# The opening of a hybrid decoder layer rebuilt: token sums from a token-major copy on ScalarE, the first two weight chunks together by quarters, one store on another queue

## The chip, the cores and the metric

The kernel runs on one core of one Trainium2 chip. The metric is device time in microseconds (us); lower is better. The core's engines are TensorE (PE; PEld is its weight load), VectorE (DVE), ScalarE (ACT), GpSimd (POOL) and SyncE (SP, which here only issues DMA). They run side by side and wait for each other by semaphores.

## The reference, cut to what matters

One layer over 272 tokens (16 learned meta tokens and 256 inputs) of width 2048, in float32:

```python
hn = rmsnorm(h_res, norm_g[l])          # x * rsqrt(mean(x*x) + eps) * g, token by token
p = hn @ w_in[l]                        # 2048 x 22528, by column blocks:
# glu_a | glu_b | conv_gate | q | k | v | ret_gate | merge_a | merge_b
y_a = conformer_branch(glu_a, glu_b, conv_gate, ...)   # glu, causal conv of 31 taps, layernorm, @ conv_out
o = retention_chunkwise(qf, kf, v)                     # 8 heads, with per-head decay
y_b = (groupnorm(o) * silu(ret_gate)) @ ret_out[l]
merged = sigmoid(merge_a) * y_a + sigmoid(merge_b) * y_b
h_res = h_res + merged @ w_out[l]
y = rmsnorm(h_res, final_norm_g)[:, N_META:]
```

## The kernel before

**Weights as a stream.** All weights pass once, as chunks of 128 x 2048 float32 (1 MB), in the order of the list `seq`. For each chunk SP loads `raw` (three buffers), `split` cuts it in two parts for a float32 product in three passes (`whi` on ScalarE and `wlo` on VectorE, three buffers each; a buffer comes free when TensorE is done with the chunk that it held), and TensorE multiplies it. A chunk of the input projection gives 128 columns for all tokens, in one PSUM bank of the pool `accp`, which has four; the bank comes free when VectorE has read it. Chunks are counted from 0 here. Chunks 0 and 1 are glu gates, 2 and 3 glu values (all four by `project`, 272 tokens, 48 matmuls), chunk 4 is the first of q (by `project_wide`).

**The input.** `x_sb` holds x with channels on the partitions, as 16 groups of 128 channels. It comes in four quarters, each with a quarter of chunk 0. `hn` is x times the gain `ng`, cut in two parts (L145 on ScalarE, L146 on VectorE). The factor per token, rsqrt(mean of squares), is not in `hn`: it is multiplied in when a product is read from PSUM, from the tile `row`.

**The factor per token** is made beside the first chunks: squares on ScalarE (L154), sums over 16 groups on VectorE (L155, L158, `part`), sums over partitions as three small products with `ones` (`token_sums`, L172), the power -1/2 on GpSimd (L103, `rcol`). `token_row` spreads it over all partitions by products with `ident` (L183, L184), copies it to `row` (L185) and multiplies the rotary table `cs_sb` with it (L186). What reads the products of chunks 0 to 2 from PSUM (`evac`, for chunk 0 the line L265) is held back until then:

```python
        evac = seq[i][1](*parts.pop(i))
        if i < 3:
            held.append(evac)
        ...
        elif i == 2:
            token_row()
            ...
            for evac in held:
                evac()
```

**Order.** A scheduler places the instructions of each engine, near the order of the code; every engine then runs its own list in that order, and an instruction that waits holds up all that stand behind it on its engine. At the end `finish` scales two blocks of 128 tokens and stores each in four pieces from SP (L661).

Of the kernel before, what the change touches and what calls it, by code (L numbers as in the profile page):

```python
# [10 lines left out]
F32 = mybir.dt.float32  # L11
# [25 lines left out]
def hybrid_kernel(ctx: ExitStack, tc, xt, xnat, gain, par, fg, cs, dec, win, cout, rout, wout, out):  # L37
# [78 lines left out]
    x_sb = xin.tile([P, KT, L], F32, name="x_sb")  # L116
    sq = xin.tile([P, KT, L], F32, name="sq")
    part = xin.tile([P, CH, L], F32, name="part")
# [4 lines left out]

    def pre_norm():
        """x * g, transposed and split; the first chunk of weights; the sums of squares."""
        hi = stage.tile([P, D], F32R, tag="whi", name="whi", bufs=SPLITS)
        lo = stage.tile([P, D], F32R, tag="wlo", name="wlo", bufs=SPLITS)
        parts[0] = (hi, lo)
        raw = raws[0] = stage.tile([P, D], F32, tag="raw", name="raw", bufs=LOADS)
        n = KT // CH  # L130
        for c in range(CH):
            s = slice(c * n, (c + 1) * n)
            nc.sync.dma_start(out=x_sb[:, s], in_=xt[:, s])
            w = slice(c * 512, (c + 1) * 512)
            nc.sync.dma_start(out=raw[:, w], in_=seq[0][0][:, w])
        load(1, 2)
        nc.sync.dma_start(out=par_sb, in_=par)
        nc.sync.dma_start(out=cs_sb, in_=cs)
        for i in range(2, LOADS):
            load(i)  # L140
        for c in range(CH):
            s = slice(c * n, (c + 1) * n)
            w = slice(c * 512, (c + 1) * 512)
            for k in range(c * n, (c + 1) * n):
                nc.scalar.activation(out=hn_hi[:, k], in_=x_sb[:, k], func=AF.Copy, scale=ng[:, k:k + 1])  # L145
                nc.vector.scalar_tensor_tensor(out=hn_lo[:, k], in0=x_sb[:, k], scalar=ng[:, k:k + 1],  # L146
                                               in1=hn_hi[:, k].bitcast(F32), op0=ALU.mult, op1=ALU.subtract)
            split(raw[:, w], hi[:, w], lo[:, w])
        raws.pop(0)

    def part_sums():
        n = KT // CH
        for c in range(CH):
            nc.scalar.activation(out=sq[:, c * n:(c + 1) * n], in_=x_sb[:, c * n:(c + 1) * n], func=AF.Square)  # L154
            nc.vector.tensor_reduce(out=part[:, c], in_=sq[:, c * n:(c + 1) * n].rearrange("p k t -> p t k"),  # L155
                                    op=ALU.add, axis=mybir.AxisListType.X)
            if c:
                nc.vector.tensor_tensor(out=part[:, 0], in0=part[:, 0], in1=part[:, c], op=ALU.add)  # L158

    def last32(pool, a, n):  # L160
        """The last 32 tokens of a, three times over."""
# [4 lines left out]

    def token_sums():
# [5 lines left out]
        nc.gpsimd.memset(cols, 1.0)  # L173
# [3 lines left out]
        for t in range(3):  # L177
            nc.vector.tensor_copy(out=lhs[:, t], in_=rcol[:, t:t + 1].broadcast_to([P, P]))
# [10 lines left out]
    def project(acc, hi, lo, group=KT):  # L189
        """acc[:, :L] = (128 columns of the chunk).T @ input, all tokens."""  # L190
        for c in range(0, KT, group):
            for k in range(c, c + group):
                w = hi[:, k * P:(k + 1) * P]
                nc.tensor.matmul(acc[:, 0:L], lhsT=w, rhs=hn_hi[:, k], start=(k == 0), stop=False)  # L194
                nc.tensor.matmul(acc[:, 0:L], lhsT=w, rhs=hn_lo[:, k], start=False, stop=False)  # L195
            for k in range(c, c + group):
                nc.tensor.matmul(acc[:, 0:L], lhsT=lo[:, k * P:(k + 1) * P], rhs=hn_hi[:, k],  # L197
                                 start=False, stop=(k == KT - 1))
# [11 lines left out]
    def halves(acc, out):  # L210
        """out = the sum of both halves of acc."""
# [4 lines left out]
    def contract(acc, hi, lo, a_hi, a_lo, kts, col):  # L216
        """acc = sum over kts of w[:, kt, col block].T @ a[:, kt]."""
# [581 lines left out]
```

## Time and the profile before

| | us |
|---|---|
| median of three runs | 1461.59 |
| lowest and highest run | 1460.44, 1461.92 |
| span of the profiled execution | 1460.0 |
| TensorE busy in it | 1441.5 |
| first matmul | 7.63 |
| first matmul of chunk 4 | 43.44 |

The profile gives the profiled execution by its span, from the first to the last instruction; what lies around the span is not shown. That span is 1.59 us under the median of the runs. Times of the trace are counted from the start of the span.

### The profile page before, as it was taken

The page shows a single profiled execution, that of the slowest core. Times are in us where ns is not written, and L with a number is a line of the kernel's source. Part 1 is how long each engine was busy: PE and PEld are TensorE (multiplying, and loading weights), DVE is VectorE, ACT ScalarE, POOL GpSimd, SP SyncE. Part 2 cuts the span into 40 slices and gives each one's busy share as a digit, 9 for nine tenths or more (in the row PEclk, how much of TensorE's full clock was granted, in tenths as well). Part 3 has the DMA queues.
Part 4 walks back from the last instruction along what each step waited for, and adds up shares of the span by engine and source line. Part 5 has one row for each costly group of instructions (what it writes and reads, how often), then busy time and mean ns, then how long its engine had stood idle before and what let it go on. Part 6 is the DMA issues. An engine that isn't in the chain of part 4 may idle for free.

```text
span 1460.0 us, 23130 instructions
## 1 busy us (share of the span) xinstructions
PE 1441.5 (99%) x9790; PEld 1339.5 (92%) x9790; DVE 1080.3 (74%) x1475; ACT 685.7 (47%) x833; POOL 9.4 (1%) x24
## 2 busy tenths in 40 slices
PE   7999999999999999999999999999999999999997
PEld 6999999999999999999999999989888888888886
DVE  7987956985895696689579569757878876666553
ACT  6445446344435534534443453454456654444433
POOL 0000000000000000000000000000000000000000
PEclk9999999999999999999999999999999999999999
DMA  7645454555455455455455455545455555555752
GB/s 267 210 164 174 173 184 171 173 178 176 154 194 173 160 176 199 149 173 199 153 174 182 172 173 173 174 155 192 173 195 180 187 188 190 186 186 189 287 177 84
DMA packets 38839, 263.38 MB, mean 180 GB/s; under 512 B 4432, under 2 KB 4432, under 8 KB 8016
## 3 DMA queue, kind: packets, MB, share of 16 engines
q1 hardware_dynamic: 37152, 256.59, 51.3%
q10 hardware_dynamic: 1584, 5.32, 1.0%
q8 instruction: 77, 1.26, 0.3%
q14 instruction: 26, 0.21, 0.0%
HBM read 259.79 MB, written 2.10 MB: 179 GB/s over the span
## 4 chain that ended last, share of the span: by engine, by line
PE 97%; DVE 1%; ACT 1%; issue 0%; DMA 0%; ACTq 0%; POOLq 0%; POOL 0%
PE ps L208 29%; PE ps L206 14%; PE ps L194 11%; PE ps L195 11%; PE ps L197 11%; PE ps L223 4%; PE ps L220 4%; PE ps L221 4%; PE ps L594 2%; PE ps L597 2%; PE ps L593 2%; PE ps L374 0%; PE ps L434 0%; ACT hn L145 0%; DVE part L155 0%; PE ps L410 0%
## 5 line engine op out<-in xcount | busy, mean ns | idle before, releaser
L51 DVE TENSOR_TENSOR wlo<-raw,whi 128x2048 fp32r<-128x2048 f32 (+2 forms) x244 | 549.9, 2254 | 171.5 <-ACT whi L50 144.8
L50 ACT ACTIVATE whi<-raw 128x2048 fp32r<-128x2048 f32 (+2 forms) x244 | 460.6, 1888 | 303.1 <-PE ps L195 122.4
L208 PE MATMUL ps<-hn,whi 128*128 128x512 f32 x1536 | 384.4, 397 | 0.0
L208 PEld LDWEIGHTS ps<-hn,whi 128*128 128x128 f32 x1536 | 285.5, 189 | 59.0
L194 PE MATMUL ps<-hn,whi 128*128 128x272 f32 x1280 | 328.9, 292 | 7.7 <-ACT whi L50 7.6
L195 PE MATMUL ps<-hn,whi 128*128 128x272 f32 x1280 | 327.3, 289 | 0.0
L194 PEld LDWEIGHTS ps<-hn,whi 128*128 128x128 f32 x1280 | 243.0, 190 | 8.1 <-ACT whi L50 8.0
L195 PEld LDWEIGHTS ps<-hn,whi 128*128 128x128 f32 x1280 | 243.2, 190 | 1.1
L252 DVE SCALAR_TENSOR_TENSOR c_sb<-u,par_sb,c_sb 128x256 f32<-128x256 f32 x480 | 205.9, 480 | 1.5
L206 PEld LDWEIGHTS ps<-hn,wlo 128*128 128x128 f32 x1536 | 194.8, 189 | 8.9
L206 PE MATMUL ps<-hn,wlo 128*128 128x256 f32 x1536 | 197.1, 282 | 0.0
L197 PE MATMUL ps<-hn,wlo 128*128 128x272 f32 x1280 | 172.7, 287 | 0.5 <-DVE wlo L51 0.4
L213 ACT COPY half<-ps 128x256 f32<-128x256 f32 x112 | 41.6, 372 | 280.1 <-PE ps L208 280.1
L197 PEld LDWEIGHTS ps<-hn,wlo 128*128 128x128 f32 x1280 | 164.4, 188 | 1.1 <-DVE wlo L51 1.1
L220 PE MATMUL ps<-zhi,whi 128*128 128x256 f32 x512 | 125.9, 280 | 0.0
L221 PE MATMUL ps<-zlo,whi 128*128 128x256 f32 x512 | 125.9, 280 | 0.0
L221 PEld LDWEIGHTS ps<-zlo,whi 128*128 128x128 f32 x512 | 96.3, 188 | 0.0
L220 PEld LDWEIGHTS ps<-zhi,whi 128*128 128x128 f32 x512 | 96.2, 188 | 0.0
L223 PE MATMUL ps<-zhi,wlo 128*128 128x256 f32 x512 | 80.9, 280 | 0.0
L223 PEld LDWEIGHTS ps<-zhi,wlo 128*128 128x128 f32 x512 | 69.1, 188 | 0.0
L208 PE MATMUL ps<-s,whi 128*128 128x512 f32 x256 | 64.7, 395 | 0.0
L208 PEld LDWEIGHTS ps<-s,whi 128*128 128x128 f32 x256 | 47.9, 188 | 10.2
(167 smaller groups left out, 1044.7 us busy)
## 6 DMA issues: line engine op xcount, KB each, us to landing
raw<-in_win_dram SPq DMA_DIRECT2D x174, 1024.0 KB, 4.9
raw<-in_rout_dram SPq DMA_DIRECT2D x32, 1024.0 KB, 4.9
raw<-in_cout_dram SPq DMA_DIRECT2D x16, 1024.0 KB, 4.9
raw<-in_wout_dram SPq DMA_DIRECT2D x16, 1024.0 KB, 4.9
x_sb<-in_xt_dram SPq DMA_DIRECT2D x4, 544.0 KB, 6.4
dec<-in_dec_dram ACTq DMA_DIRECT2D x8, 264.0 KB, 4.2
tail<-in_xnat_dram ACTq DMA_DIRECT2D x1, 2048.0 KB, 8.6
out_dram<-tail SPq DMA_DIRECT2D x8, 256.0 KB, 2.5
```

Source lines behind the costliest of these rows:

```text
L50: nc.scalar.activation(out=hi, in_=src, func=AF.Copy)
L51: nc.vector.tensor_tensor(out=lo, in0=src, in1=hi.bitcast(F32), op=ALU.subtract)
L194: nc.tensor.matmul(acc[:, 0:L], lhsT=w, rhs=hn_hi[:, k], start=(k == 0), stop=False)
L195: nc.tensor.matmul(acc[:, 0:L], lhsT=w, rhs=hn_lo[:, k], start=False, stop=False)
L197: nc.tensor.matmul(acc[:, 0:L], lhsT=lo[:, k * P:(k + 1) * P], rhs=hn_hi[:, k], start=False, stop=(k == KT - 1))
L206: nc.tensor.matmul(acc[:, 0:SEQ], lhsT=lo[:, j * P:(j + 1) * P], rhs=a[:, j, 0], start=False, stop=False)
L208: nc.tensor.matmul(both, lhsT=hi[:, k * P:(k + 1) * P], rhs=a[:, k], start=(k == 0), stop=(k == KT - 1))
L213: nc.scalar.copy(out=t, in_=acc[:, SEQ:])
L220: nc.tensor.matmul(acc, lhsT=hi[:, k, col], rhs=a_hi[:, k], start=(j == 0), stop=False)
L221: nc.tensor.matmul(acc, lhsT=hi[:, k, col], rhs=a_lo[:, k], start=False, stop=False)
L223: nc.tensor.matmul(acc, lhsT=lo[:, k, col], rhs=a_hi[:, k], start=False, stop=(j == n - 1))
L252: nc.vector.scalar_tensor_tensor(out=c, in0=u[:, t:t + SEQ], scalar=w, in1=c, op0=ALU.mult, op1=ALU.add)
```

## The change

`xrow` is a second copy of x from the host with tokens on the partitions (128, 128 and the last 32); `load_rows` loads its 2.36 MB behind chunk 3. ScalarE squares each row and adds it up in the same instruction (`accum_out`), which takes the place of the squares and sums of before; the products with `ones` go. Two small DMAs on GpSimd's queue copy the last 32 factors to two more groups of partitions. The gain rides in `x_sb` as a 273rd column, so the load of `ng` goes. Chunks 0 and 1 are loaded, cut and multiplied together, quarter by quarter (`first_pair`). Twelve 128 x 128 products of `ident` are added (`warm_up`). `token_row` comes after chunk 3, and four `evac` are held instead of three. The loads of `cs_sb` and `par_sb` move behind chunks 4 and 5. The last of the eight stores is issued by ScalarE.

```diff
-    ng = pers.tile([P, KT], F32, name="ng")
-    nc.scalar.dma_start(out=ng, in_=gain)
+    def warm_up(n):
+        ps = bank()
+        for _ in range(n):
+            nc.tensor.matmul(ps[:, 0:P], lhsT=ident, rhs=ident, start=True, stop=True)
...
         for c in range(CH):
             s = slice(c * n, (c + 1) * n)
-            nc.sync.dma_start(out=x_sb[:, s], in_=xt[:, s])
             w = slice(c * 512, (c + 1) * 512)
-            nc.sync.dma_start(out=raw[:, w], in_=seq[0][0][:, w])
-        load(1, 2)
-        nc.sync.dma_start(out=par_sb, in_=par)
-        nc.sync.dma_start(out=cs_sb, in_=cs)
+            if c == 0:
+                nc.sync.dma_start(out=x_sb[:, 0:2], in_=xt[:, 0:2])
+                nc.sync.dma_start(out=raw[0][:, w], in_=seq[0][0][:, w])
+                nc.sync.dma_start(out=x_sb[:, 2:n], in_=xt[:, 2:n])
+            else:
+                nc.sync.dma_start(out=x_sb[:, s], in_=xt[:, s])
+                nc.sync.dma_start(out=raw[0][:, w], in_=seq[0][0][:, w])
+            nc.sync.dma_start(out=raw[1][:, w], in_=seq[1][0][:, w])
...
-            split(raw[:, w], hi[:, w], lo[:, w])
+            for i in range(2):
+                split(raw[i][:, w], hi[i][:, w], lo[i][:, w])
+    def first_pair():
+        accs = [bank(accp) for _ in range(2)]
+        ws = [parts.pop(i) for i in range(2)]
...
+            for acc, (hi, lo) in zip(accs, ws):
+                project(acc, hi, lo, range(c * n, (c + 1) * n))
...
     def token_sums():
-        tots = [bank() for _ in range(3)]
-        last = last32(xin, part[:, 0:1], 1)
-        for t, a in enumerate((part[:, 0, 0:P], part[:, 0, P:2 * P], last[:, 0])):
-            n = P if t < 2 else 96
-            nc.tensor.matmul(tots[t][0:n, 0:2], lhsT=a, rhs=ones[:, 0:2], start=True, stop=True)
         nc.gpsimd.memset(cols, 1.0)
-        for t, n in enumerate((P, P, 96)):
-            nc.vector.tensor_copy(out=cols[0:n, t:t + 1], in_=tots[t][0:n, 0:1])
-        rsqrt_cols(rcol, cols, 3, 1.0)
+        for t in range(3):
+            n = P if t < 2 else 32
+            nc.scalar.activation(out=xr[0:n, t], in_=xr[0:n, t], func=AF.Square, accum_out=cols[0:n, t:t + 1])
+        rsqrt_cols(rcol, cols, 3, 1.0 / D)
+        for c in range(1, 3):
+            nc.gpsimd.dma_start(out=rcol[32 * c:32 * c + 32, 2:3], in_=rcol[0:32, 2:3])
         for t in range(3):
             nc.vector.tensor_copy(out=lhs[:, t], in_=rcol[:, t:t + 1].broadcast_to([P, P]))
...
-            nc.sync.dma_start(out=out[rows, cols], in_=h[:, t, cols])
+            queue = nc.scalar if t and c == 1 else nc.sync
+            queue.dma_start(out=out[rows, cols], in_=h[:, t, cols])
...
+    warm_up(12)
     pre_norm()
-    for i in range(1, SPLITS - 1):
-        cut(i, 2)
     held = []
+    pair = first_pair()
     for i in range(len(seq)):
         load(i + LOADS)
+        if i == 0:
+            load_rows()
+        elif i == 1:
+            nc.sync.dma_start(out=cs_sb, in_=cs)
+        elif i == 2:
+            nc.sync.dma_start(out=par_sb, in_=par)
         cut(i + SPLITS - 1)
...
-        evac = seq[i][1](*parts.pop(i))
-        if i < 3:
+        evac = seq[i][1](None, None, pair[i]) if i < 2 else seq[i][1](*parts.pop(i))
+        if i < 4:
             held.append(evac)
...
-        if i == 0:
-            part_sums()
-        elif i == 1:
+        if i == 1:
             token_sums()
-        elif i == 2:
+        elif i == 3:
             token_row()
```

On TensorE the twelve products of `ident` (L125) are first in the code. In the built program of the change the scheduler has them here, in the first quarter, `ps_184` being chunk 0 and `ps_185` chunk 1:

```order
L207 MATMUL ps_184<-hn_88,whi_116 128x272 [waits DVE_49]
L209 MATMUL ps_184<-hn_88,wlo_117 128x272 x4
L206 MATMUL ps_185<-hn_88,whi_119 128x272 [waits Activation_49]
L207 MATMUL ps_185<-hn_88,whi_119 128x272
L206 MATMUL ps_185<-hn_88,whi_119 128x272
L125 MATMUL ps_102<-ident_72 128x128 [waits Pool_49]
L125 MATMUL ps_102<-ident_72 128x128 x11
L207 MATMUL ps_185<-hn_88,whi_119 128x272
```

They stand behind the first 15 products of the weights. Before, the same place on TensorE, between the first and the second quarter of chunk 0 (`ps_175`), reads:

```order
L195 MATMUL ps_175<-hn_90,whi_105 128x272 [waits DVE_49]
L197 MATMUL ps_175<-hn_90,wlo_106 128x272 [waits DVE_49]
L197 MATMUL ps_175<-hn_90,wlo_106 128x272 x3
L194 MATMUL ps_175<-hn_90,whi_105 128x272 [waits Activation_49]
L195 MATMUL ps_175<-hn_90,whi_105 128x272 [waits DVE_49]
```

So chunk 0 followed itself there, where now a quarter of chunk 1 and the twelve products stand between two of its quarters.

The second place is the spread of the factor on TensorE. Before, it stands between chunk 2 (`ps_316`) and chunk 3 (`ps_390`):

```order
L197 MATMUL ps_316<-hn_90,wlo_172 128x272 x15
L183 MATMUL ps_365<-ident_74,lhs_102 128x128 [waits DVE_49] x2
L184 MATMUL ps_365<-ident_74,lhs_102 128x16 [waits DVE_49]
L194 MATMUL ps_390<-hn_90,whi_237 128x272 [waits Activation_49]
L195 MATMUL ps_390<-hn_90,whi_237 128x272
```

In the change it stands between chunk 3 (`ps_372`) and chunk 4 (`ps_453`), which is the fifth chunk to ask for one of the four banks:

```order
L209 MATMUL ps_372<-hn_88,wlo_295 128x272 x15
L196 MATMUL ps_421<-ident_72,lhs_99 128x128 [waits DVE_49] x2
L197 MATMUL ps_421<-ident_72,lhs_99 128x16 [waits DVE_49]
L220 MATMUL ps_453<-hn_88,whi_313 128x512 [waits DVE_49,Activation_49]
L220 MATMUL ps_453<-hn_88,whi_313 128x512 x14
```

A chunk that has a free bank stood behind the spread, and now one stands there that waits for VectorE.

The third place is VectorE around that spread in the change, where `rcol` is the factor, `lhs` its three spread columns and `sgb_431` the reading of chunk 0's bank:

```order
L100 TENSOR_SCALAR rs_302<-cols_98 128x3 [waits Activation_49,Pool_49]
L184 COPY lhs_99<-rcol_92 128x128 [waits Pool_49]
L184 COPY lhs_99<-rcol_92 128x128
L51 TENSOR_TENSOR wlo_314<-raw_291,whi_313 128x2048 [waits DMAHW2_49,PE_49,Activation_49]
L184 COPY lhs_99<-rcol_92 128x128 [waits DMASW1_49,DMASW0_49]
L198 COPY row_91<-ps_421 128x272 [waits PE_49]
L199 TENSOR_TENSOR cs_sb_71<-cs_sb_71,row_91 128x544 [waits DMAHW3_49,DVE_49]
L279 TENSOR_TENSOR sgb_431<-ps_184,row_91 128x272 [waits DMAHW7_49,DMAHW1_49,DMAHW0_49]
L51 TENSOR_TENSOR wlo_369<-raw_310,whi_368 128x2048 [waits DMAHW4_49,Activation_49]
```

The third copy to `lhs`, which waits for GpSimd's two DMAs, stands alone now, behind the low part of chunk 4. Ahead of it ScalarE runs the two casts of chunks 2 and 3 and then the three squares:

```order
L50 ACTIVATE whi_287<-raw_134 128x2048 [waits DMAHW5_49]
L50 ACTIVATE whi_294<-raw_282 128x2048 [waits DMAHW6_49,DVE_49,PE_49]
L179 ACTIVATE xr_97,cols_98<-xr_97 128x2048 [waits DMAHW7_49,Pool_49]
L179 ACTIVATE xr_97,cols_98<-xr_97 128x2048 [waits DMAHW0_49]
L179 ACTIVATE xr_97,cols_98<-xr_97 32x2048 [waits DMAHW1_49]
L50 ACTIVATE whi_313<-raw_291 128x2048 [waits DMAHW2_49,DVE_49,PE_49]
```

The cast of chunk 3, `whi_294`, waits for TensorE (its buffer is chunk 0's), and the squares stand behind it. Behind the opening the lists of TensorE, VectorE and ScalarE are the same in both programs, but for the last store.

## Rows read from the trace of the kernel before

**Rows 1.** Page of the profile, part 1: busy time of each engine.
```profile
PE 1441.5 (99%) x9790; PEld 1339.5 (92%) x9790; DVE 1080.3 (74%) x1475; ACT 685.7 (47%) x833; POOL 9.4 (1%) x24
```

**Rows 2.** Windows: length, busy PE, PEld, DVE, ACT, POOL, granted clock, DMA share, GB/s.
```profile
5.00:16.00 11.00, 8.02 (x38) 7.03 (x39) 9.82 (x19) 10.70 (x22) 0.00 (x0) 1.00 1.03 402
...
26.00:26.50 0.50, 0.00 (x0) 0.00 (x0) 0.47 (x2) 0.00 (x0) 0.00 (x0) 0.73 0.01 0
26.96:33.05 6.09, 6.09 (x27) 6.09 (x28) 4.88 (x9) 3.95 (x5) 0.87 (x1) 0.50 0.47 164
...
43.44:1452.40 1408.96, 1408.94 (x9588) 1308.64 (x9586) 1045.10 (x1423) 657.50 (x792) 6.82 (x10) 1.00 0.52 178
1455.75:1458.25 2.50, 0.00 (x0) 0.00 (x0) 0.00 (x0) 0.00 (x0) 0.00 (x0) 0.63 1.03 383
```

**Rows 3.** Timeline, TensorE, opening: start, duration (us), operation, count, idle before.
```profile
7.63 0.59 PE L194 MATMUL ps<-hn,whi 128*128 128x272 f32 x1 [7.63 <-ACT whi L50]
...
8.71 0.43 PE L194 MATMUL ps<-hn,whi 128*128 128x272 f32 x1
8.93 0.43 PE L195 MATMUL ps<-hn,whi 128*128 128x272 f32 x1
...
12.65 0.29 PE L195 MATMUL ps<-hn,whi 128*128 128x272 f32 x1
...
26.96 0.98 PE L172 MATMUL ps<-ones,part 128*128 128x2 f32 x4 [2.70 <-DVE part L158]
...
34.46 2.16 PE L197 MATMUL ps<-hn,wlo 128*128 128x272 f32 x16
36.46 0.61 PE L183 MATMUL ps<-ident,lhs 128*128 128x128 f32 x4
36.99 0.39 PE L184 MATMUL ps<-ident,lhs 32*128 32x16 f32 x2
...
43.44 0.86 PE L208 MATMUL ps<-hn,whi 128*128 128x512 f32 x3
```

**Rows 4.** Timeline, ScalarE, opening.
```profile
5.30 1.76 ACT L145 ACTIVATE hn<-x_sb,ng 128x272 fp32r<-128x272 f32 x4 [2.63 <-DMA ng<-in_gain_dram]
6.97 0.61 ACT L50 ACTIVATE whi<-raw 128x512 fp32r<-128x512 f32 x1
...
27.21 3.71 ACT L50 ACTIVATE whi<-raw 128x2048 fp32r<-128x2048 f32 x2
```

**Rows 5.** Timeline, VectorE, opening.
```profile
15.11 1.74 DVE L146 SCALAR_TENSOR_TENSOR hn<-x_sb,ng,hn 128x272 fp32r<-128x272 f32 x4
16.76 0.68 DVE L51 TENSOR_TENSOR wlo<-raw,whi 128x512 fp32r<-128x512 f32 x1
...
29.45 0.17 DVE L102 TENSOR_SCALAR rs<-cols 128x3 f32<-128x3 f32 x1
30.68 0.50 DVE L178 COPY lhs<-rcol 128x128 f32<-128x128 f32 x3 [1.06 <-POOL rcol L103]
...
37.42 0.44 DVE L185 COPY row<-ps 128x272 f32<-128x272 f32 x1 [1.84 <-PE ps L184]
37.90 0.73 DVE L186 TENSOR_TENSOR cs_sb<-cs_sb,row 128x544 f32<-128x544 f32 x1
38.54 0.78 DVE L265 TENSOR_TENSOR sgb<-ps,row 128x272 f32<-128x272 f32 x2
```

**Rows 6.** Source line 133, the four loads of x: landings.
```profile
L133 SPq DMA_DIRECT2D x_sb<-in_xt_dram x4: 387/455/738, 0.7 to 3.9; - x4
...
DMA to landing us min/median/max: 4.4/6.4/7.8
```

**Rows 7.** DMA issues: size of one, median us to landing.
```profile
out_dram<-tail SPq DMA_DIRECT2D x8, 256.0 KB, 2.5
...
tail<-in_fg_dram ACTq DMA_DIRECT2D x1, 1024.0 KB, 13.2
...
ng<-in_gain_dram ACTq DMA_DIRECT2D x1, 8.0 KB, 4.5
```

More of the change, by code (lines that the diff above doesn't have):

```diff
@@ L122, in hybrid_kernel @@
     nc.gpsimd.memset(pst.bitcast(F32), 0.0)
+    def warm_up(n):
+        ps = bank()
+        for _ in range(n):
+            nc.tensor.matmul(ps[:, 0:P], lhsT=ident, rhs=ident, start=True, stop=True)
     def pre_norm():
[L126 to L129, printed above, removed]
+        raw, hi, lo = [], [], []
+        for i in range(2):
+            raw.append(stage.tile([P, D], F32, tag="raw", name="raw", bufs=LOADS))
+            hi.append(stage.tile([P, D], F32R, tag="whi", name="whi", bufs=SPLITS))
+            lo.append(stage.tile([P, D], F32R, tag="wlo", name="wlo", bufs=SPLITS))
+            parts[i] = (hi[i], lo[i])
         n = KT // CH
@@ L141, in pre_norm, with load_rows, token_sums @@
         for c in range(CH):
-            s = slice(c * n, (c + 1) * n)
             w = slice(c * 512, (c + 1) * 512)
             for k in range(c * n, (c + 1) * n):
-                nc.scalar.activation(out=hn_hi[:, k], in_=x_sb[:, k], func=AF.Copy, scale=ng[:, k:k + 1])
-                nc.vector.scalar_tensor_tensor(out=hn_lo[:, k], in0=x_sb[:, k], scalar=ng[:, k:k + 1],
+                g = x_sb[:, k, L:L + 1]
+                nc.scalar.activation(out=hn_hi[:, k], in_=x_sb[:, k, 0:L], func=AF.Copy, scale=g)
+                nc.vector.scalar_tensor_tensor(out=hn_lo[:, k], in0=x_sb[:, k, 0:L], scalar=g,
                                                in1=hn_hi[:, k].bitcast(F32), op0=ALU.mult, op1=ALU.subtract)
-            split(raw[:, w], hi[:, w], lo[:, w])
-        raws.pop(0)
-    def part_sums():
+            for i in range(2):
+                split(raw[i][:, w], hi[i][:, w], lo[i][:, w])
+    def first_pair():
+        accs = [bank(accp) for _ in range(2)]
+        ws = [parts.pop(i) for i in range(2)]
         n = KT // CH
         for c in range(CH):
[L154 to L158, printed above, removed]
+            for acc, (hi, lo) in zip(accs, ws):
+                project(acc, hi, lo, range(c * n, (c + 1) * n))
+        return accs
+    def load_rows():
+        for t in range(3):
+            n = P if t < 2 else 32
+            nc.sync.dma_start(out=xr[0:n, t], in_=xrow[0:n, t])
+    def token_sums():
+        nc.gpsimd.memset(cols, 1.0)
+        for t in range(3):
+            n = P if t < 2 else 32
+            nc.scalar.activation(out=xr[0:n, t], in_=xr[0:n, t], func=AF.Square, accum_out=cols[0:n, t:t + 1])
+        rsqrt_cols(rcol, cols, 3, 1.0 / D)
+        for c in range(1, 3):
+            nc.gpsimd.dma_start(out=rcol[32 * c:32 * c + 32, 2:3], in_=rcol[0:32, 2:3])
+        for t in range(3):
+            nc.vector.tensor_copy(out=lhs[:, t], in_=rcol[:, t:t + 1].broadcast_to([P, P]))
     def last32(pool, a, n):
@@ L186, in token_row, with project @@
         nc.vector.tensor_tensor(out=cs_sb, in0=cs_sb, in1=row.unsqueeze(1).broadcast_to([P, 2, L]), op=ALU.mult)
[L189 to L198, printed above, removed]
+    def project(acc, hi, lo, ks=range(KT)):
+        for k in ks:
+            w = hi[:, k * P:(k + 1) * P]
+            nc.tensor.matmul(acc[:, 0:L], lhsT=w, rhs=hn_hi[:, k], start=(k == 0), stop=False)
+            nc.tensor.matmul(acc[:, 0:L], lhsT=w, rhs=hn_lo[:, k], start=False, stop=False)
+        for k in ks:
+            nc.tensor.matmul(acc[:, 0:L], lhsT=lo[:, k * P:(k + 1) * P], rhs=hn_hi[:, k],
+                             start=False, stop=(k == KT - 1))
     def project_wide(acc, hi, lo, a):
@@ L225, in proj_chunk, with use @@
     def proj_chunk(blk, n, evac):
-        def use(hi, lo):
+        def use(hi, lo, acc=None):
+            if acc is not None:
+                return lambda: evac(acc)
             acc = bank(accp)
             if n == L:
-                project(acc, hi, lo, KT // CH if blk == B0 else KT)
+                project(acc, hi, lo)
             else:
```

17 lines of the change are left out of this document (7 added, 10 removed).

## Prediction, written before the kernel ran

> **What bounds the kernel now.** I read the page's busy times first. TensorE is busy for 1441.5 of 1460.0 us, VectorE, the next, for 1080.3 [rows 1]. Next I asked the windows where the rest lies: from the start of chunk 4 to 1452.4 TensorE is busy for 1408.94 of 1408.96 us [rows 2]. Nothing there can be gained by letting TensorE wait less, and since the change leaves its list as it was behind the opening, the same 1409 us follow once chunk 4 starts. So the sum is the start of chunk 4, 43.44 now [rows 3], plus what happens behind the last product. At 0.125 us per product of 272 columns (16 in the 2.00 us from 34.46 to 36.46) four chunks of 48 need 24 us; 43.44 holds three losses.
>
> First, nothing runs until 7.63: ScalarE waits for the tiny load of the gain until 5.30, makes four casts (1.67 us) and a cast of weights (0.61) [rows 4]. Second, the engine starts at the lower of its two levels, 1.2 GHz: products come every 0.22 us (8.71, 8.93) until about 12.6 [rows 3]. Third, behind chunk 1 it idles 2.70 us for VectorE's sums [rows 3]; 2.0 us into that idling, at 26.2, the granted clock falls (0.73 over the half microsecond from 26.0) and stays at 0.50 until 33.05 [rows 2]. That costs 3.0 us more, half of 6.09.
>
> **The change, part by part.**
>
> *First product.* The first load of x is cut in half, 280 KB. The whole one, 557 KB, landed 4.4 us after its issue at 0.7, at 5.1 [rows 6]; at the opening's 402 GB/s [rows 2] half of it is there 0.7 us sooner, at 4.4. Two casts (0.84, half of 1.67) and one cast of weights (0.61) [rows 4] put the first product at 5.9. Bounds: 6.6 if the half lands no sooner than the whole did, 5.2 if it is as much better again.
>
> *Twelve products of `ident`.* They stand behind 15 products of the first quarters, so they come in the middle of the work and delay it. Two such products took 0.53 us, from 36.46 to 36.99 [rows 3], so one is 0.27 at 2.4 GHz and I take 0.53 at 1.2 GHz. The 15 ahead take 3.3 us at 0.22; with 0.3 us for the second half of x they end at 9.5. The clock rose 5.0 us after the first product (7.63 to 12.65) and 6.1 us after 26.96 the other time, so I put the rise at 5.9 + 5.5 = 11.4. Until then 3.6 of the twelve run, the other 8.4 take 2.2 us: they end at 13.6. They cost 4.1 us (bounds 3.2 and 6.4, all at one level). Nothing hides them, since the data are ahead by then: at 402 GB/s a quarter of x and two of weights, 1.08 MB, take 2.7 us, and VectorE needs 1.65 (15.11 to 16.76) and two times 0.68 [rows 5], 3.0 us, as long as TensorE's 24 products.
>
> *The pair and chunks 2 and 3.* The other 81 products of the pair take 10.1 us, to 23.7; chunks 2 and 3 take 12.0, to 35.7, at 2.4 GHz throughout, as no products with `ones` stand between. The idle 2.70 us and the fall of the clock there are gone. Ahead of need: chunks 2 and 3 come in right behind the pair (6.4 MB, at 402 GB/s by 20).
>
> *Token sums on ScalarE.* Off VectorE go four reductions and three additions; TensorE did not wait for VectorE in this stage except for them, so this is counted in the hole above. New is a chain. The cast of chunk 3 waits for chunk 0's buffer, freed twelve products before the pair's end, at 22.2; 1.86 us each for such a cast [rows 4] gives 24.1. Three squares stand behind it. Nearest row: the same cast of 2048 columns; I take 2.0 each with the reading of the sum, 30.1 in all. Their data, 2.36 MB, are there by 25.6 at 402 GB/s. From the scaling of the sums over the power to the first spread copy it was 1.23 us (29.45 to 30.68) [rows 5]: 31.3. Then GpSimd issues two DMAs of 128 bytes; at 0.4 us for an issue [rows 6] the second leaves at 31.7. No row shows GpSimd's queue. The nearest is the load of the gain, 8 KB on a queue of its own, 4.5 us; the low bound is a store, 2.5, and the high one 13.2 [rows 7]. I take 4.5, as the gain was small and alone on its queue too: 36.2, and with the copy to `lhs` 36.4. TensorE is there at 35.7, does the first two spread products until 36.2, waits 0.2, and is done with the third (0.32 [rows 3]) at 36.75. The Trainium skill (DMA: Bandwidth & Descriptors, section "Anatomy of one DMA — SWDGE (gpsimd) path") gives about 2.0 us for a small DMA on that path; by it the copies land at 33.7, off the path, and the sum would be 0.25 us lower. No row here shows it.
>
> *Four held banks.* All four banks are held now when chunk 4 wants one. TensorE must wait until VectorE has written `row`, multiplied `cs_sb` and read chunk 0's bank: from 37.42 to 38.54, and 0.39 for one of the two readings [rows 5], 1.5 us and 0.1 for the hand-over. Behind TensorE's wait stands everything. Before, chunk 3 stood there and had the fourth bank, so these three steps were hidden. Chunk 4 starts at 38.4.
>
> *Moved loads.* `cs_sb` lands behind chunk 4 of the weights (10.1 MB, about 29), `par_sb` behind chunk 5 (about 32). First needed at 37.2 and near 41; cost nothing. Without that cover each us late would be a us for `cs_sb` alone.
>
> *The store.* Issued by ScalarE, the last one need not queue behind three others on SP. Its issue time alone would promise 0.5 us, about one issue [rows 6]. But from 1455.75 to 1458.25 the DMA share is 1.03, at 383 GB/s [rows 2]: the stores are bound by bytes. The Trainium skill (Trainium Kernel Development and Optimization, section "Key Constraints") says that SP's and ScalarE's DMAs share the same 16 engines and that another issuer saves issue time only. By the rule the last byte lands when it did, by the issue alone the sum would be 0.5 lower; the DMA share agrees with the rule, and I count 0.
>
> **The sum.** 43.44 - 38.4 = 5.0 us. The profiled span is 1.59 under the median of the runs; a difference carries over, so 1461.6 - 5.0 = **1456.6**.
>
> **Rivals.**
>
> *A. The hole only moves, and the clock falls in it.* Between 35.7 and 38.4 TensorE has 0.85 us of small products and 1.8 us of idling in two pieces; before, it fell 2.0 us into one piece [rows 2]. For it: that is close, and a late copy lengthens it. Against it: the work between. If it falls, chunk 4 runs some 6 us at 1.2 GHz, 3.0 us lost: 1459.6. The change would then not do what its parts say, as the idling and the second cold stretch are both back.
>
> *B. The copies are quick and the first data early.* First product at 5.2, rise of the clock 4.9 us later, copies at 2.5 us: the pair ends at 22.7, chunk 3 at 34.7, and with 0.85 and 1.6 chunk 4 starts at 37.1: 1455.3. For it: a store landed in 2.5. Against it: the first landing is a guess from bytes, while fixed time may hold it.
>
> *C. Slower: GpSimd's copies are late.* The spread waits for both, and TensorE stands. To be over 0.2% slower, chunk 4 must start 2.9 us later than before; the clock surely falls then (3.0), so the point is a landing 5.0 us behind mine, 9.5 us after the issue. For it: a load behind others took 13.2 [rows 7], and 1 MB weights are in flight then. With 13.2 it would be 1456.6 + 8.7 + 3.0 = 1468.3. Against it: the gain landed in 4.5 while the quarters were loading.
>
> **How the numbers follow.** 0.2% of the time, 2.9 us, is about what a measurement tells from no change. My case gets 0.50 (1455.7 to 1457.8, by the bounds of the first landing, the twelve products and a quick copy), A 0.26, B 0.17, C 0.07. Faster by over 0.2% means under 1458.7: my case, B, and a mild A in which the clock comes back early (0.04), 0.71. Within 0.2%: the rest of A, 0.22. Slower: C, 0.07. The range reaches from B's low end, 1454.6, to A with a little delay, 1459.9.
>
> **What would show it.** First product at 5.9; twelve L125 products from 9.5 to 13.6, the later ones 0.27 apart; no idle stretch behind the pair, and granted clock 1.00 from there to 35.7; the two DMAs issued near 31.5 and landing near 36; an idle stretch of 1.6 us ahead of chunk 4, put down to VectorE's reading of chunk 0's bank; chunk 4 at 38.4; then no wait to the end, and 1409 us to the last product. The last store issued 0.5 us sooner and landing when it did. I am wrong if the granted clock is at 0.50 behind 38, if the copies land after 37, or if the squares wait for their rows.

## Result and profile after

The changed kernel takes 1470.63 us (median of four runs, 1469.22 to 1472.95), the kernel before 1461.01 beside it: a ratio of 1.0069, interval [1.0055, 1.0084]. It is slower, by about 9.6 us, where the prediction said 5.0 us faster. The profiled execution is the fastest of the four; its span is 1467.2 us against 1460.0, and these 7.2 us are what the traces can account for.

The page of after, part 1 (busy time of TensorE; it answers to [rows 1]):
```profile
PE 1448.0 (99%) x9808; PEld 1346.5 (92%) x9808; DVE 1072.8 (73%) x1467; ACT 688.1 (47%) x834; POOL 10.6 (1%) x26
```
TensorE is busier by 6.5 us, of which the twelve products of `ident` (L125) account for less than 3. Windows of after, columns as in [rows 2]:
```profile
13.57:35.89 22.32, 22.32 (x181) 22.32 (x180) 11.61 (x18) 16.14 (x20) 2.05 (x3) 1.00 0.91 357
35.89:42.01 6.12, 1.20 (x8) 0.93 (x7) 3.19 (x6) 1.99 (x2) 0.00 (x0) 0.71 0.90 313
...
42.01:45.00 2.99, 2.99 (x7) 2.43 (x8) 2.99 (x4) 2.32 (x3) 0.00 (x0) 0.50 0.18 65
...
42.01:1459.40 1417.39, 1417.38 (x9586) 1316.79 (x9586) 1049.60 (x1428) 659.86 (x794) 6.84 (x10) 1.00 0.51 177
```
The first row is what was hoped for: 22.32 us without a gap at the full clock. The last is the surprise. From the start of chunk 4 to the last product there is still no idle time, and yet it lasts 1417.39 us where the kernel before needed 1408.96 [rows 2].

The opening on TensorE in after (timeline, as [rows 3]):
```profile
5.35 0.60 PE L206 MATMUL ps<-hn,whi 128*128 128x272 f32 x1 [5.35 <-ACT whi L50]
...
7.79 0.60 PE L206 MATMUL ps<-hn,whi 128*128 128x272 f32 x1 [1.16 <-ACT hn L153]
...
10.75 3.06 PE L125 MATMUL ps<-ident 128*128 128x128 f32 x24
13.57 0.37 PE L207 MATMUL ps<-hn,whi 128*128 128x272 f32 x1
...
35.89 0.61 PE L196 MATMUL ps<-ident,lhs 128*128 128x128 f32 x4
39.67 0.60 PE L197 MATMUL ps<-ident,lhs 32*128 32x16 f32 x2 [3.18 <-DVE lhs L184]
42.01 5.25 PE L220 MATMUL ps<-hn,whi 128*128 128x512 f32 x15 [1.74 <-DVE sgb L279]
```
Chunk 3 ends at 35.89, then TensorE stands 3.18 us for `lhs` and 1.74 for the bank, and chunk 4 begins at 42.01, 1.4 us ahead of before [rows 3], at the clock's lower level. ScalarE's part of the chain in after:
```profile
23.70 1.92 ACT L50 ACTIVATE whi<-raw 128x2048 fp32r<-128x2048 f32 x1 [2.67 <-DMA raw<-in_win_dram]
26.16 1.92 ACT L179 ACTIVATE xr<-xr 128x2048 f32<-128x2048 f32 x1 [0.54 <-DMA xr<-in_xrow_dram]
...
29.16 1.92 ACT L179 ACTIVATE xr<-xr 128x2048 f32<-128x2048 f32 x1 [0.99 <-DMA xr<-in_xrow_dram]
...
31.07 1.90 ACT L179 ACTIVATE xr<-xr 32x2048 f32<-32x2048 f32 x1
```
VectorE's:
```profile
33.16 0.17 DVE L100 TENSOR_SCALAR rs<-cols 128x3 f32<-128x3 f32 x1 [5.21 <-ACT xr L179]
34.33 0.36 DVE L184 COPY lhs<-rcol 128x128 f32<-128x128 f32 x2 [1.00 <-POOL rcol L101]
...
39.39 0.23 DVE L184 COPY lhs<-rcol 128x128 f32<-128x128 f32 x1 [2.20 <-DMA rcol<-rcol]
40.31 0.44 DVE L198 COPY row<-ps 128x272 f32<-128x272 f32 x1 [0.70 <-PE ps L197]
```
The two transfers that the third copy waits for, on GpSimd's queue (duration of the issue, first and last start, time to landing):
```profile
L182 POOL DMA_DIRECT2D rcol<-rcol x2: 502/588/674, 34.6 to 35.3; - x2
...
DMA to landing us min/median/max: 4.0/4.3/4.5
```
On SP's queue, the issues ahead of the token-major rows:
```profile
10.56 8.29 SPq L67 DMA_DIRECT2D raw<-in_win_dram  x2
18.89 2.06 SPq L172 DMA_DIRECT2D xr<-in_xrow_dram  x3
```
The first of these rows is two loads of weights: the one at 10.56 takes 0.33 us, and the next, chunk 3's, is issued only at 18.52, after a wait of 7.6 us for a free buffer. The rows of `xr` stand behind it and could be issued only at 18.89.

**Where the 7.2 us arise.** Both kernels issue the same products behind chunk 4, so the start of the same product can be set against itself. After minus before is -1.43 us at chunk 4, +0.17 at 57 us, and then it grows without a single wait: +1.33 at 261 us, +3.49 at 528, +5.45 at 798, +7.19 at 1087, +7.54 at 1190, about its highest, and +7.01 at 1452 (times of before). So: -1.4 from the earlier start, +1.6 from the cold clock, +6.8 from products that take longer, +0.2 behind the last product. One tile shows the growth in the profile itself: the product of `ve` and `pe` comes once in each of the eight heads (view of the tile `pe`: first and last start). Before, then after:
```profile
L413 PE MATMUL ps<-ve,pe x8: 397/398/398, 111.3 to 970.6; 96*128 96x512 f32 x8
```
```profile
L427 PE MATMUL ps<-ve,pe x8: 397/397/397, 111.7 to 977.1; 96*128 96x512 f32 x8
```
Seven heads take 859.3 us before and 865.4 after. Products grouped by shape, from 60 to 1445 us, say which (count | busy us, mean ns of one). Before:
```profile
L220 PE MATMUL ps<-zhi,whi 128*128 128x256 f32 x512 | 125.9, 280 | 0.0
...
L223 PE MATMUL ps<-zhi,wlo 128*128 128x256 f32 x512 | 80.9, 280 | 0.0
```
After:
```profile
L209 PE MATMUL ps<-hn,wlo 128*128 128x272 f32 x1208 | 164.3, 288 | 0.0
L232 PE MATMUL ps<-zhi,whi 128*128 128x256 f32 x512 | 128.6, 285 | 0.0
...
L235 PE MATMUL ps<-zhi,wlo 128*128 128x256 f32 x512 | 82.0, 282 | 0.0
```
A row's mean contains the overlap with the next product, so the experiments use the distance from one start to the next. The largest differences, as mean distance before and after: `zhi,whi` 117.3 and 122.9 ns, `zhi,wlo` 117.3 and 119.7, `hn,wlo` of 272 columns 123.8 and 125.8. These are the same instructions on the same data, 1.6 to 4.8 per cent slower. Over all kinds, count times change of the mean distance adds up to 6.8 us, the whole growth.

### The profile page after: what moved, and what is told of

Same layout as the page of the kernel before. It is cut to its first block, busy times and chain, and to the rows that moved or that the text cites. A ratio compares the mean times of both kernels' runs of the same rounds, so it can differ in the third digit from the quotient of the medians.

```text
span 1467.2 us, 23170 instructions
## 1 busy us (share of the span) xinstructions
PE 1448.0 (99%) x9808; PEld 1346.5 (92%) x9808; DVE 1072.8 (73%) x1467; ACT 688.1 (47%) x834; POOL 10.6 (1%) x26
## 4 chain that ended last, share of the span: by engine, by line
PE 96%; DMA 2%; ACT 1%; issue 1%; DVE 0%; SPq 0%; POOL 0%; POOLq 0%; DVEq 0%
PE ps L220 29%; PE ps L218 14%; PE ps L207 10%; PE ps L209 10%; PE ps L206 10%; PE ps L232 4%; PE ps L235 4%; PE ps L233 4%; PE ps L607 2%; PE ps L611 2%; PE ps L608 2%; DMA xr<-in_xrow_dram 1%; DMA x_sb<-in_xt_dram 1%; PE ps L388 0%; PE ps L448 0%
## 5 line engine op out<-in xcount | busy, mean ns | idle before, releaser
L51 DVE TENSOR_TENSOR wlo<-raw,whi 128x2048 fp32r<-128x2048 f32 (+1 forms) x246 | 549.8, 2236 | 179.2 <-ACT whi L50 126.1
L50 ACT ACTIVATE whi<-raw 128x2048 fp32r<-128x2048 f32 (+1 forms) x246 | 460.9, 1875 | 312.6 <-PE ps L207 127.7
```

The costliest lines, as they stand in the source:

```text
L50: nc.scalar.activation(out=hi, in_=src, func=AF.Copy)
L51: nc.vector.tensor_tensor(out=lo, in0=src, in1=hi.bitcast(F32), op=ALU.subtract)
```

## Experiments

What the change does to these products that its diff hardly shows: `ng`, 64 bytes a partition, stood ahead of `ident` in the persistent pool. The gain now travels with `x_sb`, so `ng` is gone, and every tile allocated behind it lies 64 bytes lower. The addresses are read from the two built programs: `hn` 98304 before and 98240 after, `zhi` 220192 and 220128. The staging pool changed too: `raw` is now asked for first, so that `raw`, `whi` and `wlo` changed places (all still 128 above a multiple of 256).

**Four kernels on the addresses.** First, the 64 bytes alone:
```diff
+    pers.tile([P, KT], F32, name="pad")
     ident = pers.tile([P, P], F32, name="ident")
```


> The changed kernel with an unused tile of 64 bytes a partition in the place that the norm weights ng had, so that every tile allocated behind it (ident to hn, the retention's and the final phase's) lies at its old address again; the three staging tags (raw, whi, wlo) keep the new order. Theory A, the shift by 64 bytes makes TensorE's reads slower: the 7 us that the two traces drift apart between 60 and 1100 us are gone, 1463.4. Theory B, the exchanged places of raw, whi and wlo in the staging pool do it: unchanged, 1470.6. Theory C, neither (the phase of the other engines against TensorE, the PSUM banks, or the GpSimd queue): 1470.6.

Second, the staging order alone:
```diff
-            raw.append(stage.tile([P, D], F32, tag="raw", ...))
             hi.append(stage.tile([P, D], F32R, tag="whi", ...))
             lo.append(stage.tile([P, D], F32R, tag="wlo", ...))
+            raw.append(stage.tile([P, D], F32, tag="raw", ...))
```


> The changed kernel with the first tiles of the staging pool asked for in the old order (whi, wlo, raw in place of raw, whi, wlo), which puts the three tags back at their old addresses; everything behind stays shifted by 64 bytes. Theory A (shift): 1470.6. Theory B (staging order): 1463.4. Theory C (neither): 1470.6.

Third, both:

> Both edits together: all addresses as before, but for the tiles of the opening's own pool. Theories A and B: 1463.4 each, of which the opening explains 2 and noise the rest. Theory C (neither): 1470.6. If the two effects add, this one gains the sum of what the two single edits gain.

Fourth, the kernel before with the new staging order:
```diff
+        raw = raws[0] = stage.tile([P, D], F32, tag="raw", ...)
         hi = stage.tile([P, D], F32R, tag="whi", ...)
         lo = stage.tile([P, D], F32R, tag="wlo", ...)
-        raw = raws[0] = stage.tile([P, D], F32, tag="raw", ...)
```


> The kernel before with one line moved: raw is asked for ahead of whi and wlo, so that the three staging tags lie as in the changed kernel; not one instruction differs. Theory A (shift): 1461.0, unchanged. Theory B (staging order): the drift appears without any other part of the change, 1468. Theory C (neither): 1461.0.

Measured, beside 1460.59 for the kernel before: 1463.77 with the 64 bytes (ratio 1.0022 [1.0012, 1.0031]), 1471.05 with the order (1.0070 [1.0055, 1.0085]), 1463.78 with both (1.0018 [1.0008, 1.0028]), 1460.61 for the fourth (0.9996 [0.9987, 1.0006]). The 64 unused bytes give back 7 us; the staging order does nothing. In the trace with the 64 bytes the same product lies +1.78 us against before at 57 us and +1.78 at 1452: the drift is not reduced, it is gone to the hundredth of a microsecond. The tile `pe` in that trace (972.4 - 113.1 is 859.3 again):
```profile
L428 PE MATMUL ps<-ve,pe x8: 397/398/398, 113.1 to 972.4; 96*128 96x512 f32 x8
```

**Which tiles.** The unused bytes placed behind `hn` in place of ahead of `ident`:
```diff
     hn = pers.tile([P, KT, 2, L], F32R, name="hn")
     ...
+    pers.tile([P, KT], F32, name="pad")
     c_sb = pers.tile([P, NB, SEQ], F32, tag="cm", name="c_sb")
```


> The changed kernel with the unused 64 bytes placed behind hn instead of ahead of ident: ident, ones and hn (the normed input, the moving operand of the projections) stay shifted by 64 bytes, every tile behind it (zhi, zlo, s, m and the rest) is back at its old address. If TensorE's time hangs on the address of each moving operand by itself, the cost by kinds of product in the trace of the changed kernel gives the answer: the zhi, zlo and s products take back 4.5 us, the hn products keep 2.3 us, so 1466.1. If hn alone does it: 1470.6. If only the tiles behind hn do: 1463.8.

Measured 1468.1 (1.0049 [1.0034, 1.0064]), between the theories. With `hn` still shifted the drift from 57 to 1452 us is 4.6. The `hn` products take what they take in the changed kernel (125.8 ns for `hn,wlo`). The z products, back at their old address, take 118.5 ns where they took 117.3: better than 120.0 on average, but not restored. So both groups of tiles matter, and the adding up by kinds was off by 2 us: the z products took 118.5 ns at an address at which they take 117.3 elsewhere, so the start address of its own operand doesn't fix a product's time alone.

**The products by themselves.** A kernel with nothing else in it, addresses swept in steps of 16 bytes:
```diff
+            nc.tensor.matmul(dst, lhsT=w[:, woff + k * P:woff + (k + 1) * P], rhs=rhs,
+                             start=(i == 0), stop=(i == n - 1))
...
+            for o in range(16):
...
+                sweep(REPS, parts, 0, 4 * o)
```


> Not the computation: nothing but 48 products in a row at each of 16 start addresses (steps of 16 bytes, 0 to 240 modulo 256) of the moving operand, for 272 and 256 columns and for twice 256 columns, then of the stationary operand, then with two moving addresses in turn; first with the other engines idle, then with ScalarE, VectorE and weight transfers at work. The output is zeros. Theory A1, the start address of the moving operand alone sets the time of a product: the mean spacing differs by 3 to 8 ns of some 120 between addresses, in the idle and in the busy half alike. Theory A2, the address matters only where other engines use the same memory: no difference in the idle half, some in the busy half. Theory A3, the stationary operand's address: the sweep of the weights shows the difference and the sweep of the moving operand does not.

In the trace the two halves came out the other way round. The work of the other engines does not wait for TensorE's products, so it ran from the start to 324 us, beside the first half's sweeps of the moving operand. Everything behind it, the whole second half (from 530 us) included, ran alone (page, part 2: busy share in tenths, 40 slices of the span of 1023.7 us):
```profile
PE   5999999999999999999999999999999999999999
...
DVE  7566665666664000000000000000000000000000
ACT  7999999999997000000000000000000000000000
...
DMA  8887887878883000000000000000000000000000
```
The sweep of 272 columns ran at 38 to 134 us and again at 530 to 626, that of 256 columns at 134 to 225 and at 627 to 717, so each has one turn with the others at work and one without. The sweep of the weights had both its turns behind 324 us. The mean distance between starts, worked out from the trace without the first four products of each sweep (ns, weights at 128 modulo 256):
```
moving operand at (mod 256)    0    32    64    96   128   160   192   224   240
256 columns, rest busy      118.5 117.3 113.3 118.4 120.0 116.7 117.8 120.0 113.3
256 columns, rest idle      118.5 117.3 113.3 118.4 120.0 116.7 117.8 120.0 113.3
272 columns, rest busy      126.6 123.8 123.3 126.7 125.4 125.8 126.7 126.7 123.3
```
Theory A1 holds but for its word "alone": the moving operand's address makes up to 6.7 ns of 120, and to 0.1 ns the same whether ScalarE, VectorE and transfers work or not, so it is no contention with them (A2). The kernel's addresses are in this table: `zhi` at 32 takes 117.3 in both, and 224, where the change puts it, gives 120.0, which is the mean of the three z kinds in after (122.9, 119.7, 117.4). A3 is half right: the sweep of the weights, with the moving operand held at 160, runs over the same range, 113.3 to 120.1. Whether the other engines change that sweep was not measured.

That made a test which needs nothing of the change, the kernel before with `zhi` and `zlo` moved from 32 to 64:
```diff
+        if h == 0:
+            ret.tile([P, 8], F32, tag="zpad", name="zpad")
         hi = ret.tile([P, 4, SEQ], F32R, tag="zhi", name="zhi")
```


> The kernel before, with one unused tile of 32 bytes a partition ahead of zhi, so that zhi and zlo start 64 bytes behind a multiple of 256 and not 32; nothing else moves, and no instruction differs. In the run of products alone, 256 columns took 117.3 ns at 32 and 113.3 at 64 with the same weights' address, and 117.3 is what these 1536 products take in the kernel before. Theory A1 (addresses alone set a product's time): 1536 times 4.0 ns less, 6.1 us, 1454.4. Theory R, the 7 us came from something that went along with the address (the order in which tiles are handed out, the neighbours of hn): unchanged, 1460.5.

Measured 1455.33 against 1460.63 (0.9964 [0.9952, 0.9977]): 32 unused bytes and no other difference, 5.3 us faster. In its groups by shape:
```profile
L220 PE MATMUL ps<-zhi,whi 128*128 128x256 f32 x512 | 123.1, 277 | 0.0
...
L223 PE MATMUL ps<-zhi,wlo 128*128 128x256 f32 x512 | 79.1, 277 | 0.0
```
The distance between starts is 114.0 where the table said 113.3; over 1536 products that is 1.1 us, about the 0.8 us by which the forecast of the gain was too high. The kernel's own sequences, alone:

> Not the computation: the kernel's own sequences of products (a chunk of 272 columns with high, low, high parts; a wide chunk; a retention chunk; a chunk of the merge) at 16 start addresses of the moving operand each, in steps of 16 bytes, the first two also with rows 2304 bytes apart in place of 2176; weights at the kernel's address modulo 256; nothing else runs and the output is zeros. If a product's time hangs on addresses alone, the sequences at the addresses of the kernel before take what they take there (124.9 ns a product in the chunk of 272 columns, 117.3 in the retention chunk), those at addresses 64 bytes less take what the changed kernel shows (125.9 and 120.0), and the retention chunk at 64 takes 113.3. If the rest of the kernel has a part in it, they come out alike at both.

The length of a chunk, from its first start to that of the next, in its last repeats at an address:
```
start (mod 256)                  0    16    32    64    96   112   160   192   224   240
chunk of 272 columns, us     5.987 5.973 5.993 6.053 6.013 6.047 5.987 6.033 6.000 6.016
wide chunk, us               5.613 5.631 5.580 5.627 5.606 5.560 5.600 5.633 5.613 5.553
retention chunk, us          5.695 5.691 5.630 5.440 5.680 5.621 5.600 5.440 5.760 5.440
merge chunk, us              5.612 5.627 5.646 5.547 5.627 5.640 5.600 5.483 5.653 5.553
```
The merge chunk at 112 is its first repeat: its second is the last chunk of the program, nothing starts behind it, and from its first to its last start it is 5.426, one product short. Repeats of one chunk at one address can differ (the merge chunk at 192 took 5.559 and 5.483), so a few hundredths of a microsecond are within the scatter.

Most is as expected on addresses alone: at before's `hn` (0) 124.7 ns a product against 124.9 expected, at the changed one (192) 125.7 against 125.9; the retention chunk 117.3, 120.0 and 113.3 at 32, 224 and 64. The wide chunk doesn't fit: alone it takes 0.02 us more at 192 than at 0, in the kernels its products of 512 columns went from 234.7 to 233.9 ns, 1.3 us less over the 1504 of them. What makes the drift is settled: the address shift, through the products themselves.

**The opening.** With the drift taken out, the opening of the changed kernel is 3.2 us *slower* than the kernel before in the medians (1.8 in the traces at the same product), so a second thing went wrong. The third copy to `lhs`, of 32 rows, put ahead of the two transfers:
```diff
-        for c in range(1, 3):
-            nc.gpsimd.dma_start(out=rcol[32 * c:32 * c + 32, 2:3], in_=rcol[0:32, 2:3])
         for t in range(3):
-            nc.vector.tensor_copy(out=lhs[:, t], in_=rcol[:, t:t + 1].broadcast_to([P, P]))
+            n = P if t < 2 else 32
+            nc.vector.tensor_copy(out=lhs[0:n, t], in_=rcol[0:n, t:t + 1].broadcast_to([n, P]))
+        for c in range(1, 3):
+            nc.gpsimd.dma_start(out=rcol[32 * c:32 * c + 32, 2:3], in_=rcol[0:32, 2:3])
```


> The changed kernel with the 64 bytes back, and the copy of the last 32 tokens into lhs cut to the 32 rows that the product reads and issued ahead of GpSimd's two small transfers, so that the row product no longer waits for them. Theory 1, the wait of 3.2 to 4.3 us ahead of the row product hangs on these transfers alone: the row product follows chunk 3 at once and chunk 4 starts 3 to 4 us earlier, 1459.6; with the clock then staying high another 1.5, 1458.1. Theory 2, something else on the chain (squares, casts ahead of them) is as late: 1463.8, with the wait named after another releaser.

Measured 1460.26 (0.9993 [0.9984, 1.0002]), 3.5 us under the kernel with the 64 bytes: theory 1. Its profiled execution, 1457.88, is among the fastest of ten. The waits on TensorE in it (us in total, times, longest) name no `lhs` any more, but a cast of weights, queued on ScalarE behind the load of `dec`, which waits for the row product:
```profile
PE ps L208 <- ACT whi L50: 5.4, 1, 5.4
PE ps L222 <- ACT whi L50: 2.5, 1, 2.5
```
Next, `load_rows()` ahead of the loop, `token_sums()` at i == 0 and `token_row()` at i == 2:
```diff
     pair = first_pair()
+    load_rows()
...
-        if i == 1:
+        if i == 0:
             token_sums()
-        elif i == 3:
+        elif i == 2:
             token_row()
```


> As the run on lhs, with the token-major rows loaded ahead of the fourth chunk of weights, their squares ahead of the cast of chunk 3, and the row product between chunks 2 and 3, so that the pair and chunk 2 are evacuated while chunk 3 runs. If the opening is bounded by the token chain and by TensorE's hole behind chunk 3: no hole, chunk 4 starts at 36.9 instead of 43.4 in the kernel before, and the whole comes to 1454.0, faster than both. If the rows loaded early delay the weights of chunk 2 or 3 by as much as they save, TensorE waits for whi or wlo instead: 1458 to 1464.

Measured 1457.15 (0.9977 [0.9968, 0.9987]): faster than the kernel before, by half of what was expected. Issued at 10.6 in place of 18.9, the rows landed no sooner than 12.2 to 15.2 us later, among the weights. The profiled execution is the slowest of the ten, 1460.74; in it the hole came back ahead of chunk 3, with the clock down behind it:
```profile
32.06 1.22 PE L198 MATMUL ps<-ident,lhs 128*128 128x128 f32 x4 [2.78 <-DVE lhs L184]
...
34.37 0.43 PE L208 MATMUL ps<-hn,whi 128*128 128x272 f32 x1
34.59 0.43 PE L209 MATMUL ps<-hn,whi 128*128 128x272 f32 x1
...
38.73 0.29 PE L208 MATMUL ps<-hn,whi 128*128 128x272 f32 x1
38.86 0.29 PE L209 MATMUL ps<-hn,whi 128*128 128x272 f32 x1
```
The products are 0.22 us apart for four microseconds and 0.13 after. The granted clock is 0.50 from 31.7 to 38.5, with TensorE busy for 6.4 us of it, so this execution lost some 3 us to the clock. Most of the ten did not lose as much: eight took 1456.2 to 1457.7, at a mean granted clock of 0.998 or 0.999 against 0.996 here. So the fall of the clock explains the profiled execution and not the median; the last run below has the same opening, and its profiled execution, 1446.93, is close to its median.

**Both together.** The kernel before with three chosen addresses, the tile `zpad` of the run on z (not repeated here) and these two:
```diff
-    hn = pers.tile([P, KT, 2, L], F32R, name="hn")
+    hn = pers.tile([P, KT * 2 * L + 64], F32R, name="hn")
+    hn = hn[:, 60:60 + KT * 2 * L].rearrange("p (k h t) -> p k h t", k=KT, h=2)
...
-        fin["s"] = fp.tile([P, NB, 2, SEQ], F32R, tag="s", name="s")
+        sm = fp.tile([P, NB * 2 * SEQ + 64], F32R, tag="s", name="s")
+        fin["s"] = sm[:, 52:52 + NB * 2 * SEQ].rearrange("p (k h t) -> p k h t", k=NB, h=2)
```


> The kernel before with three start addresses chosen from the sequences measured alone, and not one instruction more or less: zhi and zlo at 64 modulo 256 as in the run on z, hn at 240 in place of 0, s (the merge's operand) at 112 in place of 160. From the sequences: 94 wide chunks times -0.060 us, 75 chunks of 272 columns times +0.029, 16 chunks of the merge times -0.174, and -5.3 as measured for z: -5.6 + 2.2 - 2.8 - 5.3 = -11.5, so 1449. If the sequences alone don't carry over to hn, whose chunks of both kinds alternate in the kernel: between 1455.3 (z alone) and 1452.5 (z and s).

And the same with the opening of the run on rows early:

> The run on rows early (the changed kernel with its 64 bytes back, lhs ahead of GpSimd's transfers, the token rows loaded early and the row product ahead of chunk 3) with the same three start addresses. If the opening and the addresses are independent, the gains add: 1457.2 - 11.5 = 1445.7, or 1449 to 1452 if hn's addresses don't carry over; if the new opening's gain depended on the old addresses, it is no faster than the kernel before with the addresses alone.

Measured, beside 1460.56: 1451.77 (0.9936 [0.9919, 0.9953]) and 1447.18 (0.9911 [0.9897, 0.9926]). From the distances in the trace of the first, times their counts: wide `hn` products -7.5 us (expected -5.6), 272 columns +2.1 (+2.2), z -5.3 (-5.3), and `s` +0.6 where -2.8 was expected. The last expectation came from the 5.426 of the merge chunk at 112, the length without its last product. With 5.640 it is 16 times +0.04, +0.6, as measured: 112 is no better for `s` than 160. The sum is then -8.1 and the forecast 1452.5, which is within 0.7 us of the measured median. The second run is the fastest of the study, 13.4 us under the kernel before; the gains of the opening (3.4) and of the addresses (8.8) make 12.2, so they add, within 1.2 us. Its waits on TensorE:
```profile
PE ps L209 <- ACT whi L50: 5.2, 1, 5.2
PE ps L199 <- DVE lhs L185: 1.4, 1, 1.4
PE ps L209 <- ACT hn L155: 1.0, 1, 1.0
```
and its windows, columns as in [rows 2]:
```profile
0.00:36.00 36.00, 28.43 (x204) 27.50 (x205) 18.94 (x35) 25.25 (x38) 3.21 (x15) 1.00 0.91 327
36.00:42.00 6.00, 6.00 (x38) 5.37 (x37) 6.00 (x7) 2.95 (x4) 0.00 (x0) 1.00 0.82 259
```
Here the clock does not fall, and chunk 4 starts at 38.28, 1.4 us behind the 36.9 expected of this opening, which is the wait for `lhs`. The rest of what the run on rows early missed isn't shown to have one cause; one part is that the opening of the kernel before isn't equally long each time: chunk 4 starts at 43.44 in its trace, and at 43.52, 41.52 and 43.41 in the traces of the three runs that leave its instructions as they are.

## Why the prediction was wrong

Two steps failed, each of them large enough to use up the 5.0 us.

- **"The same 1409 us follow once chunk 4 starts."** This step failed. The list of instructions was the same, none waited, and it took 1417.39 us: 1.6 us of the difference is the cold clock in chunk 4, and 6.8 us is products that take longer. The argument took a product's time from the trace as a property of its shape; the runs show it to depend on its operands' addresses too, and the removal of a 64-byte tile moved them all (7 us in the medians). None of the rivals held this.
- **The opening, 5.0 us faster.** This step failed as well: with the old addresses back, the changed kernel is 3.2 us slower than the kernel before (1463.77 against 1460.59). The points below take it apart, and the chain of the token sums is where it went wrong.
- **First product, 5.9.** It started at 5.35, near the low bound of 5.2. The next two slices of x weren't there, though, and TensorE's wait of 1.16 for them took half a microsecond more than the 0.55 that was gained.
- **Twelve products of `ident`, 9.5 to 13.6.** They ran from 10.75 to 13.57, 2.8 us in place of 4.1: the clock rose just after they began, and at the higher level one took 0.22 us, not 0.27. The pair ended at 23.82 (23.7) and chunk 3 at 35.89 (35.7), with the full clock and without the hole behind the pair, as predicted. That the times agree to 0.2 us is luck: the products began 1.25 us late and took 1.3 us less than forecast.
- **Squares done at 30.1.** They were done at 33.1, and this is the first size that was wrong in the chain. Two sets of data that I had "ahead of need" weren't: the weights of chunk 3 (ScalarE waited 2.67 us) and the rows (0.54 and 0.99). I had counted bytes at 402 GB/s and overlooked that SP's queue stands: the fourth load of weights has to wait for the first of three buffers, and the rows are issued behind it, at 18.89.
- **Copies issued by 31.7, landing 4.5 later.** The landing was right, 4.0 to 4.5 us. The Trainium skill's 2.0 for this path (DMA: Bandwidth & Descriptors, "Anatomy of one DMA — SWDGE (gpsimd) path") isn't what this trace shows, and the measurement decides. The issues were at 34.6 and 35.3 and took 0.5 and 0.67 us, not 0.4. `lhs` was ready at 39.6 and not 36.4. The run on `lhs` shows that this dependence cost 3.5 us of the whole and that the product never needed it.
- **Bank wait of 1.6.** It was 1.74.
- **Chunk 4 at 38.4.** It started at 42.01: the 3.0 us of the squares and the rest of the transfers' issue. Even that is an early case. In the four other traces of this opening (the 64 bytes, the order, both, and the bytes behind `hn`) chunk 4 starts at 43.41, 42.41, 43.30 and 43.27, about where it starts in the kernel before.
- **Rival A** came true as a mechanism: the granted clock is 0.71 over the hole and 0.50 from 42.01 to 45.00. It cost 1.6 us here and not 3.0 (chunk 4 took 7.2 us in place of 5.6), so that chunk 5 began at the same time in both traces. In the four other traces of this opening chunk 4 took 7.4 to 8.1 us, and chunk 5 began 1.4 to 2.0 us later than before.
- **The store, 0.** From the end of the last product to the end of the span it is 7.79 us in place of 7.58, in the kernel with the 64 bytes too. The 0.5 us of issue time weren't gained.

In the sum of the two traces: -1.4 (predicted -5.0), +1.6 for the clock, +6.8 for the addresses, +0.2 behind the last product: the 7.2 us between the spans. The profiled execution lies 1.4 us under the median of after, that of before 0.6 over its own, and this makes most of the rest to 9.6. In the medians it is 3.2 us for the opening and the end, and some 7 for the addresses.

## What to carry to other kernels

Before a stage is called unchanged because its instructions are, compare the addresses of its operands: a tile removed, resized or asked for in another order moves all that are allocated behind it, and where TensorE is busy throughout, half a per cent on every product is half a per cent of the time. The sign of such a loss in a trace is a drift that grows steadily with no wait anywhere; setting the starts of the same instructions against each other shows it, and an unused tile in the old place proves it. On the opening: follow each load back to the queue that issues it, and ask which wait for a buffer stands ahead of it, before its bytes are divided by a bandwidth. And before a trace is taken for the median, compare its time with the other executions: here the openings of the same instructions differed by up to 2 us.

## What was unexpected of the hardware

With the weights at 128 modulo 256, a product of 256 columns took from 113.3 ns (moving operand at 64 or 240) to 120.0 (at 128 or 224), with every other engine idle; a sweep of the weights' address showed the same range. That the other engines made no difference agrees with the Trainium skill (SBUF — State Buffer, section "Who interferes with whom"), which has TensorE wait on nobody there. A trace repeats itself: with equal addresses, 9500 products kept their distance to the hundredth of a microsecond over 1400 us.

Three things stay open. The runs give the times at the addresses tried, not the reason. The start address modulo 256 doesn't fix a product's time alone: z at one and the same address took 117.3 ns in one kernel and 118.5 in another in which only `hn` and the tiles ahead of it lay elsewhere, and 192 gave 117.8 in the sweep and 113.3 in the retention chunk. What else counts, the products before it for one, was not tested. And whether rows of `hn` 2304 bytes apart, of which a wide chunk took 5.54 us alone at 80 modulo 256, would carry over was not tried in the kernel.
